# A down projection by seven half-sized products, its inputs combined while the up projection runs

## The chip, the cores and the metric

The kernel runs on one core of a Trainium2 chip. The metric is the device time of one execution in microseconds. The kernel before takes 2623.7 us, the median of 3 runs (2622.65 to 2625.96).

## What is computed

Two transformer blocks on 1024 tokens of 1024 features, float32. The first has a short-convolution layer and a stick-breaking attention layer, the second a sliding-window and a differential attention and then a feed-forward part. The change touches the end of the second block, D_FF = 2816:

```python
def _conv_ffn(h, w_up, conv_w, conv_b, w_down):
    u = h @ w_up
    a, g = jnp.split(u, 2, axis=-1)
    s = a.shape[1]
    ap = jnp.pad(a, ((0, 0), (CONV_WIDTH - 1, 0), (0, 0)))
    a = ap[:, 0:s] * conv_w[0] + ap[:, 1:s + 1] * conv_w[1] + ap[:, 2:s + 2] * conv_w[2] + conv_b
    return (jax.nn.gelu(a, approximate=False) * g) @ w_down
...
        h2 = _rmsnorm(x, norm2_g[l]) * (1.0 + scale2) + shift2
        x = x + gate2 * _conv_ffn(h2, w_up[l], conv_w[l], conv_b[l], w_down[l])
    return _rmsnorm(x, final_g)
```

## The kernel before

Activations lie feature-major: a tile is 128 features by 512 tokens, and there are two halves of tokens. Every operand of a projection is split into a high and a low part of type fp32r, so that one block product is three matrix products (high by high, high by low, low by high). Weights come in pieces of up to four 128 x 128 blocks: `Piece.load` fetches one on SP's queue (tile wr), `split_h` makes the high part on ACT (wh), `split_l` the low part on DVE (wl). All pieces stand in one list, `stream`, and `advance` (line 360) keeps loads, high and low parts a set number of pieces ahead of the piece in use: 5, 3 and 2, and 8, 5 and 4 in the down projection.

The order of all instructions is made beforehand by a planner written in the kernel, `Sched`: a main program on TensorE and side tasks (generators), each resumed when the planner's own clock says that what it waits for is there. Each engine and each DMA queue then works through its list in that order. `bank` hands out the eight PSUM banks, `big` and `sml` the tiles of two pools in SBUF (34 tiles of 4 KB and 32 of 2 KB a partition), and `room` (line 311) makes a task wait until a large tile is free by the planner's count.

The up projection is already made by seven products in place of eight (`up_first`, `up_rest`, line 1543). For it, `weight_sums` (line 1435) forms sums of quarters of the up weights in memory by accumulating DMAs on POOL's queue, one every 6 us of the planner's clock from 130 us on, with a pause from 600 to 880; each has a small copy ahead of it (tile paced) that reads the newest low part of a weight piece, and so keeps the DMA from running ahead of its place. `up_out` (line 1459) makes the convolution, the gelu (tile fa) and the product with the gate, and stores each result (22 feature blocks by 2 halves) to act_d by POOL's queue.

The down projection is eight half products in the plain way. `act_side` (line 1622) loads the inputs back (tile al, five ahead) and splits them into act; `res_jobs` (line 764) takes one output block of 128 features after the other, over 22 inner blocks: the first half of the tokens 512 wide, the second half in two passes of 256 tokens, so that the last output can start early. Each result is multiplied by the gate and added to the old x (tile xn). `final` (line 1640) transposes finished blocks (yt), sums squares (fj), and after the eighth block scales and writes the output rows (y).

## Time and profile before

| | |
|---|---|
| median of 3 runs | 2623.7 us |
| the profiled execution | 2622.0 us, of which the span of instructions is 2620.2 us |
| TensorE busy (products) | 2563.2 us, 98% |
| DVE busy | 1724.2 us, 66% |
| ACT busy | 1238.8 us, 47% |
| POOL busy | 333.0 us, 13% |
| mean granted TensorE clock | 0.996 of full speed |
| HBM read and written | 213 GB/s over the span |

The span is the time from the first to the last instruction of one profiled execution. Busy time is the time in which an engine had an instruction at work; products on TensorE overlap, so their durations add up to more than the time that they take together, and the spacing of their starts is what counts.

### The profile page before, as it was taken

To read this page: it belongs to the slowest core of one execution; us is meant where nothing else is said; L and a number is where in the kernel's file an instruction comes from. 1 tells how busy PE (TensorE), PEld (TensorE's weight loads), DVE (VectorE), ACT (ScalarE), POOL (GpSimd) and SP (SyncE) were. 2 spreads that over 40 slices of the span, in tenths; PEclk is the share of its full clock that TensorE was granted. 3 is DMA by queue.
4 is the path that set the end of the run, shared out by engine and by line. 5 is a ranking of instruction groups with operands and counts; after the bars stand their busy time and mean duration, and the time that the engine had idled before them with its cause. 6 is when DMAs were issued, how large, how long until landed. Compare 5 with 4: busy or idle time off the path is not lost.

```text
span 2620.2 us, 39902 instructions
## 1 busy us (share of the span) xinstructions
PE 2563.2 (98%) x14015; PEld 2118.3 (81%) x14015; DVE 1724.2 (66%) x3137; ACT 1238.8 (47%) x2498; POOL 333.0 (13%) x598
## 2 busy tenths in 40 slices
PE   7999999999999899999999999999999999999998
PEld 6888888889877677788778887888787788887898
DVE  7866666765466777977677456674657766763564
ACT  5311113542255667667675353565535444442443
POOL 0011112332100012322200110000001000000000
PEclk9999999999999999999999999999999999999999
DMA  8866878798776656875974758555454545545675
GB/s 278 263 190 208 213 218 286 210 285 263 240 200 191 212 173 143 241 241 147 245 200 126 231 152 226 164 157 168 154 162 154 169 145 178 163 126 168 191 230 156
DMA packets 536305, 515.19 MB, mean 197 GB/s; under 512 B 30110, under 2 KB 429736, under 8 KB 536104
## 3 DMA queue, kind: packets, MB, share of 16 engines
q1 hardware_dynamic: 497396, 377.27, 49.5%
q0 software_dynamic: 36352, 131.15, 16.7%
q10 hardware_dynamic: 2356, 4.21, 0.4%
q8 instruction: 111, 1.82, 0.3%
q14 instruction: 90, 0.74, 0.1%
HBM read 422.33 MB, written 136.31 MB: 213 GB/s over the span
## 4 chain that ended last, share of the span: by engine, by line
PE 87%; DVE 6%; issue 3%; DMA 2%; ACT 1%; SPq 0%; POOL 0%; DVEq 0%; ACTq 0%; POOLq 0%
PE pj L248 70%; PE z L248 4%; PE o L248 4%; PE pv L248 4%; PE tr L249 3%; DVE om L249 2%; DVE wl L249 1%; DVE be L249 1%; PE sm L249 1%; DVE act L249 1%; DMA wr<-in_b_w_qz_dram 1%; DVE t L249 0%; DMA wr<-in_b_w_out_dram 0%; DVE p L249 0%; SPq L249 0%
## 5 line engine op out<-in xcount | busy, mean ns | idle before, releaser
L248 PE MATMUL pj<-act,wh 128*128 128x512 f32 (+1 forms) x6064 | 1831.8, 386 | 6.7 <-DVE act L249 4.2
L248 PEld LDWEIGHTS pj<-act,wh 128*128 128x128 f32 x6064 | 1094.3, 189 | 221.5 <-DVE act L249 6.3
L248 PE MATMUL pj<-act,wl 128*128 128x512 f32 (+1 forms) x3032 | 1156.5, 381 | 1.4 <-DVE wl L249 1.4
L248 PEld LDWEIGHTS pj<-act,wl 128*128 128x128 f32 x3032 | 570.2, 188 | 122.5 <-DVE wl L249 2.7
L249 DVE TENSOR_TENSOR wl<-wr,wh 128x512 fp32r<-128x512 f32 (+1 forms) x752 | 494.5, 676 | 179.8 <-ACT wh L249 172.6
L249 ACT CAST wh<-wr 128x512 fp32r<-128x512 f32 (+1 forms) x752 | 445.4, 615 | 164.6 <-PE pj L248 83.5
L249 ACT COPY aT<-tr 128x512 f32<-128x512 f32 (+3 forms) x272 | 128.3, 501 | 163.7 <-PE tr L249 159.7
L248 PE MATMUL z<-kd,qs 128*128 128x256 f32 (+2 forms) x704 | 164.3, 351 | 0.1
L249 DVE SCALAR_TENSOR_TENSOR acc<-mw,silu_c,acc 128x512 f32<-128x512 f32 x196 | 146.6, 748 | 3.1 <-DMA mw<-in_a_mod_w_dram 0.3
L248 PE MATMUL pv<-wh,act 128*128 128x256 f32 x768 | 140.3, 282 | 0.0
L249 POOL COPY paced<-wl 128x1 f32<-128x1 f32 x128 | 67.2, 525 | 512.0 <-DVE wl L249 490.0
L248 PEld LDWEIGHTS z<-kd,qs 128*128 128x128 f32 x704 | 115.0, 192 | 17.1 <-issue 5.8
L249 DVE TENSOR_TENSOR_SCAN om<-om 128x640 f32<-128x640 f32 (+3 forms) x64 | 120.8, 1887 | 9.0 <-ACT om L249 9.0
L248 PEld LDWEIGHTS pv<-wh,act 128*128 128x128 f32 x768 | 119.1, 188 | 0.3
L249 DVE SCALAR_TENSOR_TENSOR xn<-pj,mod,xo 128x512 f32<-128x512 f32 (+1 forms) x40 | 25.7, 643 | 141.2 <-PE pj L248 141.2
L248 PEld LDWEIGHTS o<-aT,vp 128*64 128x64 f32 (+1 forms) x1440 | 97.5, 147 | 23.4 <-issue 12.6
L248 PE MATMUL o<-aT,vp 128*64 128x128 f32 (+1 forms) x1440 | 114.0, 278 | 1.7 <-ACT aT L249 1.7
L248 PE MATMUL pv<-wl,act 128*128 128x256 f32 x384 | 108.0, 281 | 0.3 <-DVE wl L249 0.3
L249 ACT ACTIVATE p<-p,t 128x256 f32<-128x256 f32 (+7 forms) x128 | 81.3, 636 | 22.5 <-DVE t L249 22.4
L249 ACT COPY u<-pj 128x512 f32<-128x512 f32 x38 | 22.3, 587 | 136.7 <-PE pj L248 69.9
L249 ACT ACTIVATE om<-z 128x384 f32<-128x384 f32 (+2 forms) x128 | 68.9, 539 | 22.3 <-PE z L248 22.0
L249 PE MATMUL tr<-ident,be 128*128 128x128 f32 x416 | 61.0, 281 | 18.2 <-DVE be L249 16.9
(226 smaller groups left out, 2408.6 us busy)
## 6 DMA issues: line engine op xcount, KB each, us to landing
wr<-in_w_in_dram SPq DMA_DIRECT2D x136, 256.0 KB
mw<-in_w_ada_dram SPq DMA_DIRECT2D x96, 256.0 KB
wr<-in_w_down_dram SPq DMA_DIRECT2D x96, 256.0 KB
wr<-in_a_w_in_dram SPq DMA_DIRECT2D x80, 256.0 KB
wr<-in_w_up_dram SPq DMA_DIRECT2D x66, 256.0 KB
wr<-in_b_w_qz_dram SPq DMA_DIRECT2D x64, 256.0 KB
qs<-q_d SPq DMA_DIRECT2D x64, 256.0 KB
mw<-in_a_mod_w_dram SPq DMA_DIRECT2D x48, 256.0 KB
```

The lines of the kernel that those rows point to most:

```text
L248: return f(out, *value, **kw)
L249: return f(out=out, **kw)
```

## The change

With the token halves 0 and 1, the inner halves 0 and 1 (11 feature blocks each) and the output halves 0 and 1 (4 blocks each), the down projection needs eight block products. The change forms seven (Strassen's scheme in Winograd's form). The seven inputs are stored in dn_d: kinds 0, 1 and 6 are results of `up_out` as they are; kinds 2 to 5 are sums and differences of four of them, made by the new side task `down_in` as soon as the three later ones of a block exist, by four DVE operations (the first input, long stored, is loaded back as dT). Four sums of weight quarters, sw_d, are made by `weight_sums` after those of the up weights, by 64 more DMAs of 176 x 512 numbers (352 KB, as before). `down` then runs the products in the order of `todo`: each over 4 output blocks and 11 inner blocks, the first six 512 tokens wide, the seventh in two passes of 256. Products 0 and 1, 2 to 4, and 5 and 6 share a PSUM bank for each output block, where they add up; partial results are taken out by DVE with the gate (or its negative) and the old x. The old `final` becomes three parts, called when four, seven and eight blocks of an output are there. Inputs are freed and split kind by kind (`act_side`; `N_DOWN` large tiles are kept for results that stay). Over the whole program there are 264 products of 256 columns where there were 1056, and 8304 of 512 columns in the projections where there were 8040.

```diff
-R_SUM = 64
 AHEAD_ACT = 5
+N_DOWN = 13
...
-    act_d = scratch("act_d", [NF, 128, S])
+    dn_d = [scratch(f"dn_d{i}", [NM, 128, HT]) for i in range(7)]
     s1_d = scratch("s1_d", [2, NM, 128, HT])
     sg_d = [[scratch(f"sg_d{i}{w}", [512, HF]) for w in "ag"] for i in range(4)]
+    sw_d = [scratch(f"sw_d{i}", [HF, 512]) for i in range(4)]
...
+    w_down = w_down_2[0]
+
     def weight_sums():
-        def W(k, f, n):
-            return w_up[512 * k:512 * k + 512, n * DFF + f * HF:n * DFF + (f + 1) * HF]
+        def up(n):
+            return lambda k, f: w_up[512 * k:512 * k + 512, n * DFF + f * HF:n * DFF + (f + 1) * HF]
+
+        def down(k, f):
+            return w_down[HF * k:HF * k + HF, 512 * f:512 * f + 512]
         paced = const.tile([128, 1], F32, name="paced")
         while sch.t < T_SUM:
             yield 2.0
-        for n in range(2):
-            g = [sg_d[i][n] for i in range(4)]
-            for to, of, op in ((0, W(0, 1, n), None), (2, W(0, 0, n), None), (0, W(1, 1, n), ALU.add),
-                               (2, W(0, 1, n), ALU.add), (1, W(0, 0, n), None), (3, W(1, 0, n), None),
+        for W, g in [(up(n), [sg_d[i][n] for i in range(4)]) for n in range(2)] + [(down, sw_d)]:
+            rows, width = g[0].shape
+            step = rows // 8
+            for to, of, op in ((0, W(0, 1), None), (2, W(0, 0), None), (0, W(1, 1), ALU.add),
+                               (2, W(0, 1), ALU.add), (1, W(0, 0), None), (3, W(1, 0), None),
                                (1, g[0], ALU.add), (3, g[1], ALU.add)):
-                for r in range(0, 512, R_SUM):
-                    kw = {"accum_op": op, "max_dma_last_dim": HF * 4} if op else {}
+                for r in range(0, rows, step):
+                    kw = {"accum_op": op, "max_dma_last_dim": width * 4} if op else {}
                     while BUSY_SUM[0] < sch.t < BUSY_SUM[1]:
                         yield 2.0
                     pol.tensor_copy(out=paced, in_=f32(stream[done_to["l"] - 1].l[:, 0, 0:1]))
-                    pol.dma_start(out=g[to][r:r + R_SUM], in_=of[r:r + R_SUM], **kw)
+                    pol.dma_start(out=g[to][r:r + step], in_=of[r:r + step], **kw)
                     yield E_SUM
     fhalo = const.tile([128, NF, 2], F32, name="fhalo")
     st_f = {}
+    st_d = {}
+
+    def down_in(i, h):
+
+        t1 = sml(name="dT1")
+        syn.dma_start(out=t1, in_=dn_d[0][i])
+        h01, h10, h11 = h[0, 1], h[1, 0], h[1, 1]
+        yield t1, h01, h10, h11
+        stt = vec.scalar_tensor_tensor
+        vec.tensor_tensor(out=t1, in0=t1, in1=h01, op=ALU.subtract)
+        vec.tensor_tensor(out=h01, in0=h11, in1=h01, op=ALU.subtract)
+        yield 0.5
+        t2 = sml(name="dT2")
+        stt(out=t2, in0=h11, scalar=-1.0, in1=t1, op0=ALU.mult, op1=ALU.subtract)
+        yield t2
+        t4 = sml(name="dT4")
+        stt(out=t4, in0=t2, scalar=-1.0, in1=h10, op0=ALU.mult, op1=ALU.subtract)
+        yield t4
+        for kind, t in ((2, t2), (3, h01), (4, t4), (5, t1)):
+            store(dn_d[kind][i], t)
+            flags.add(("dn", kind, i))
...
-            store(act_d[f, :, hs(half)], t)
-            flags.add(("act", f, half))
+            i = f % NM
+            if (f // NM, half) != (0, 1):
+                kind = {(0, 0): 0, (1, 0): 1, (1, 1): 6}[f // NM, half]
+                store(dn_d[kind][i], t)
+                flags.add(("dn", kind, i))
+            if (f // NM, half) != (0, 0):
+                got = st_d.setdefault(i, {})
+                got[f // NM, half] = t
+                if len(got) == 3:
+                    sch.spawn(down_in(i, st_d.pop(i)))
...
-    DOWN = [(0, 4), (NM, 4), (4, 4), (NM + 4, 4), (8, 3), (NM + 8, 3)]
-
-    def act_side(half):
-
-        fs = [f + i for f, n in DOWN for i in range(n)]
+
+
+    def act_side():
+
+        todo = [(kind, i) for kind in range(7) for i in range(NM)]
         got = {}
-        for k in range(NF + AHEAD_ACT):
-            if k < NF:
-                yield from wait(("act", fs[k], half))
-                got[k] = sml(name="al")
-                syn.dma_start(out=got[k], in_=act_d[fs[k], :, hs(half)])
-            if k >= AHEAD_ACT:
-                t = got.pop(k - AHEAD_ACT)
+        for n in range(len(todo) + AHEAD_ACT):
+            if n < len(todo):
+                yield from wait(("dn",) + todo[n])
+                got[n] = sml(name="al")
+                syn.dma_start(out=got[n], in_=dn_d[todo[n][0]][todo[n][1]])
+            if n >= AHEAD_ACT:
+                kind, i = todo[n - AHEAD_ACT]
+                t = got.pop(n - AHEAD_ACT)
                 yield t
+                if (kind, i) == (1, 0):
+                    yield from room(1, N_DOWN)
                 yield from room(1)
-                sch.spawn(split_to(("act", k - AHEAD_ACT, half), t))
+                sch.spawn(split_to(("dn", kind, i), t))
             yield 0.6
+    def down():
+        def of(s, j):
+            src, k0, c0 = [(w_down, 0, 0), (w_down, NM, 0), (sw_d[1], 0, 0), (sw_d[2], 0, 0), (w_down, NM, 512),
+                           (sw_d[0], 0, 0), (sw_d[3], 0, 0)][s]
+            return [Piece(src, k0 + k, n, c0 + j * 128, 128) for k, n in ((0, 4), (4, 4), (8, 3))]
+
+        todo = [(s, j, 0, HT, of(s, j)) for s in range(6) for j in range(4)]
+        todo += [(6, j, c0, 256, of(6, j)) for c0 in (0, 256) for j in range(4)]
+        for t in todo:
+            stream.extend(t[4])
+        stt = vec.scalar_tensor_tensor
+
+        def multiply(ps, pieces, kind, c, start, last):
+            k = 0
+            for pc in pieces:
+                use(pc)
+                for i in range(pc.nk):
+                    a = act_of(("dn", kind, k))
+                    sch.turn(sch.when((a, pc.h, pc.l)))
+                    first = start and k == 0
+                    for n, (w, x) in enumerate(((pc.h, 0), (pc.h, 1), (pc.l, 0))):
+                        mm(ps, lhsT=w[:, i, :], rhs=a[:, x, c], start=first and n == 0, stop=k == NM - 1 and n == 2,
+                           skip_group_check=not start)
+                    if last:
+                        del A["dn", kind, k]
+                        free()
+                    k += 1
+
+        two = {}
+
+        def old(f, half):
+            if (f // 2, half) not in two:
+                two[f // 2, half] = big([2, HT], name="xo", held=True)
+            t = two[f // 2, half][:, f % 2, :]
+            syn.dma_start(out=t, in_=x4_d[f, :, hs(half)])
+            return t
+
+        def scaled(out, ps, f, minus, plus):
+
+            g = V["gt2n" if minus else "gt2"][:, f:f + 1]
+            stt(out=out, in0=ps, scalar=g, in1=plus, op0=ALU.mult, op1=ALU.add)
+
+        def run():
+            V["gt2n"] = const.tile([128, 8], F32, name="gt2n")
+            vec.tensor_scalar(out=V["gt2n"], in0=V["gt2"], scalar1=-1.0, scalar2=None, op0=ALU.mult)
+            b, s1, zo, vo = {}, {}, {}, {}
+            xs = {0: [None] * 8, 1: [None] * 8}
+
+            def after(s, j, c0, xo):
+                ps = b[j]
+                if s == 0:
+                    s1[j] = copied(ps, "s1")
+                elif s == 2:
+                    vec.tensor_tensor(out=ps, in0=ps, in1=s1[j], op=ALU.add)
+                    yield xo
+                    scaled(xo, ps, j, False, xo)
+                    sch.keep(ps)
+                    zo[j] = xo
+                elif s == 3:
+                    yield xo
+                    scaled(xo, ps, 4 + j, True, xo)
+                    sch.keep(ps)
+                    vo[j] = xo
+                else:
+                    f, half, minus, plus = {1: (j, 0, False, xo), 4: (4 + j, 0, True, xo), 5: (4 + j, 1, True, vo.get(j)),
+                                            6: (j, 1, False, zo.get(j))}[s]
+                    if s == 6:
+                        x = sml(256, name="xn")
+                        scaled(x, ps[:, c0:c0 + 256], f, minus, plus[:, c0:c0 + 256])
+                        if c0 == 0:
+                            sch.keep(ps)
+                    else:
+                        x = plus
+                        scaled(x, ps, f, minus, plus)
+                        if s == 5:
+                            sch.keep(ps)
+                    xs[half][f] = x
+                    bs = range(4) if s != 6 else range(c0 // 128, c0 // 128 + 2)
+                    yield x
+                    if s in (1, 5) and j == 3:
+                        yield from final_a(half, xs[half], 4 * (s == 5))
+                    elif s in (4, 6) and j == 2:
+                        yield from final_b(half, xs[half], 4 * (s == 4), bs)
+                    elif s in (4, 6) and j == 3:
+                        yield from final_c(half, xs[half], 4 * (s == 4), bs)
+
+            for s, j, c0, w, pieces in todo:
+                old_of = {1: (j, 0), 2: (j, 1), 3: (4 + j, 1), 4: (4 + j, 0)}.get(s)
+                xo = old(*old_of) if old_of else None
+                start = s in (0, 2, 5)
+                if start:
+                    sch.turn(sch.bank_time())
+                    b[j] = bank("pj")
+                multiply(b[j][:, c0:c0 + w], pieces, s, slice(c0, c0 + w), start, j == 3 and c0 + w == HT)
+                then(after(s, j, c0, xo))
+        return run
+
...
+    def final_a(half, xs, f0):
+
+        f = final_state(half)
+        for b in range(4):
+            yield from sch.a_bank()
+            f["ps"][b] = bank("yt")
+            final_turn(f, xs, range(f0, f0 + 4), b, 0, 0)
+            f["y"][b] = big([D], name="y", held=True)
+            c = slice(f0 * 128, f0 * 128 + 512)
+            vec.tensor_tensor(out=f["y"][b][:, c], in0=f["ps"][b], in1=fin["g"][:, c], op=ALU.mult)
+
+    def final_b(half, xs, f0, bs):
+        f = final_state(half)
+        for b in bs:
+            yield from sch.a_bank()
+            f["ps"][b] = bank("yt")
+            final_turn(f, xs, range(f0, f0 + 3), b, bs[0] if len(bs) == 2 else 0, 1)
+
...
-    last = res_jobs(w_down_2[0], "act", "gt2", x4_d, None, final, ks=DOWN, squares=False)
-    run_last = [alone(last, 0)] + [alone(again(last), (1, c0, 256)) for c0 in (0, 256)]
+    run_last = down()
...
-        sch.spawn(act_side(0))
+        sch.spawn(act_side())
         run_up1()
-        sch.spawn(act_side(1), 60.0)
         ahead.update(load=AHEAD_LOAD + E_L, h=AHEAD_H + E_H, l=AHEAD_L + E_H)
-        for run in run_last:
-            run()
+        run_last()
```

What moves, first on SP's queue in one round of the up stage (wr are weight pieces, s1l a stored partial result, al an input of the down projection; dn_d_108 holds kind 1, dn_d_107 kind 0). Before:

```order
L249 DMA wr_21967<-sg_d3a 128x4x128
L249 DMA al_21983<-act_d 128x512
L249 DMA wr_21993<-sg_d2g 128x4x128
L249 DMA wr_22015<-sg_d0g 128x4x128
L249 DMA wr_22038<-sg_d1a 128x4x128
L249 DMA s1l_22059<-s_d 128x512
```

and now:

```order
L249 DMA wr_21918<-sg_d3a 128x4x128
L249 DMA al_21934<-dn_d_108 128x512
L249 DMA wr_21944<-sg_d2g 128x4x128
L249 DMA dT_4778_21964<-dn_d_107 128x512
L249 DMA wr_21967<-sg_d0g 128x4x128
L249 DMA wr_21990<-sg_d1a 128x4x128
L249 DMA s1l_22013<-s_d 128x512
```

The load of dT stands between the first weight pieces of the round, two places behind that of al.

On DVE in a round of the same stage (fa are results of the up projection, pj PSUM banks, u and v copies of them), before:

```order
L249 TENSOR_TENSOR pj_21645<-pj_21645,u_21567 128x512
L249 TENSOR_TENSOR fa_21617<-fa_21617,pj_21645 128x512
L249 TENSOR_TENSOR act_21740<-al_20790,act_21740 128x512
L249 TENSOR_TENSOR wl_21747<-wr_21669,wh_21714 128x512
L249 TENSOR_TENSOR act_21754<-al_21026,act_21754 128x512
L249 TENSOR_TENSOR act_21762<-al_21258,act_21762 128x512
L249 TENSOR_TENSOR act_21770<-al_21493,act_21770 128x512
L249 TENSOR_TENSOR wl_21784<-wr_21692,wh_21745 128x512
L249 TENSOR_TENSOR y_4767_21798<-pj_21779,v_21776 128x512
L249 TENSOR_TENSOR wl_21807<-wr_21712,wh_21782 128x512
L249 TENSOR_TENSOR pj_21802<-pj_21802,s1l_21569 128x512
```

and now:

```order
L249 TENSOR_TENSOR pj_21847<-pj_21847,u_21765 128x512
L249 TENSOR_TENSOR fa_21819<-fa_21819,pj_21847 128x512
L249 TENSOR_TENSOR wl_21948<-wr_21874,wh_21920 128x512
L249 TENSOR_TENSOR wl_21971<-wr_21898,wh_21946 128x512
L249 TENSOR_TENSOR y_4783_21985<-pj_21966,v_21962 128x512
L249 TENSOR_TENSOR wl_21994<-wr_21918,wh_21969 128x512
L249 TENSOR_TENSOR dT_4778_21964<-dT_4778_21964,fa_21819 128x512
L249 TENSOR_TENSOR fa_21819<-fa_21741,fa_21819 128x512
L249 TENSOR_TENSOR pj_21989<-pj_21989,s1l_21767 128x512
L249 TENSOR_TENSOR wl_22019<-wr_21944,wh_21992 128x512
```

The splits of act have gone from here, and the operations on dT (and fa from two fa) stand ahead of the addition of s1l, behind y.

On POOL's queue in mid-kernel, where the second block's first projections store keys and queries (ka_d, qa_d), before:

```order
L249 DMA g_d<-gt_15084 128x512
L249 DMA g_d<-gt_15125 128x512
L249 DMA ka_d<-ks_15165 128x512
L249 DMA ka_d<-ks_15166 128x512
L249 DMA qa_d<-qh_15255 128x512
L249 DMA qa_d<-ql_15256 128x512
L249 DMA qa_d<-qh_15298 128x512
```

and now:

```order
L249 DMA g_d<-gt_15175 128x512
L249 COPY paced<-wl_15226 128x1
L249 DMA sw_d_123<-in_w_down_dram 176x512
L249 DMA ka_d<-ks_15217 128x512
L249 DMA ka_d<-ks_15218 128x512
L249 COPY paced<-wl_15295 128x1
L249 DMA sw_d_123<-in_w_down_dram 176x512
L249 DMA qa_d<-qh_15311 128x512
L249 DMA qa_d<-ql_15312 128x512
L249 COPY paced<-wl_15340 128x1
L249 DMA sw_d_123<-in_w_down_dram 176x512
```

A paced copy and a DMA of the sums stand between the stores.

## Rows read from the trace of the kernel before

**Rows 1.** The page: busy times of the engines, and POOL's DMA queue.

```profile
PE 2563.2 (98%) x14015; PEld 2118.3 (81%) x14015; DVE 1724.2 (66%) x3137; ACT 1238.8 (47%) x2498; POOL 333.0 (13%) x598
...
q0 software_dynamic: 36352, 131.15, 16.7%
```

**Rows 2.** The chain of waits, 2040 to 2621 us: start, length, what.

```profile
2051.93 304.05 PE pj L248 x1308
...
2421.99 46.01 PE pj L248 x198
...
2484.79 31.19 PE pj L248 x264
```

**Rows 3.** Groups by shape, 2356 to 2611 us: busy us, mean ns, idle before.

```profile
L248 PE MATMUL pj<-act,wh 128*128 128x256 f32 x704 | 125.6, 281 | 0.0
L248 PE MATMUL pj<-act,wh 128*128 128x512 f32 x352 | 111.0, 395 | 0.4 <-DVE act L249 0.3
...
L248 PE MATMUL pj<-act,wl 128*128 128x256 f32 x352 | 98.8, 281 | 0.0
L248 PE MATMUL pj<-act,wl 128*128 128x512 f32 x176 | 69.4, 394 | 0.0
L249 DVE TENSOR_TENSOR wl<-wr,wh 128x512 fp32r<-128x512 f32 x94 | 59.8, 684 | 7.6 <-ACT wh L249 5.7 <-PE pj L248 1.9
...
L249 DVE SCALAR_TENSOR_TENSOR xn<-pj,mod,xo 128x256 f32<-128x256 f32 x15 | 7.2, 482 | 42.7 <-PE pj L248 42.7
```

**Rows 4.** Windows: length, busy us (instructions) by engine, clock, DMA share, GB/s.

```profile
300.00:600.00 300.00, 299.66 (x1391) 246.01 (x1390) 205.59 (x336) 102.81 (x178) 74.20 (x138) 1.00 0.86 250
900.00:1200.00 300.00, 284.36 (x2052) 232.35 (x2053) 242.19 (x285) 207.65 (x451) 70.84 (x108) 0.99 0.67 186
1260.00:1320.00 60.00, 60.00 (x372) 49.00 (x371) 37.09 (x120) 31.59 (x88) 17.58 (x34) 1.00 1.03 261
1320.00:1760.00 440.00, 434.70 (x2324) 359.92 (x2323) 292.08 (x737) 236.58 (x498) 35.98 (x65) 1.00 0.62 179
1440.00:1500.00 60.00, 60.00 (x300) 50.29 (x299) 29.81 (x46) 21.85 (x39) 10.95 (x20) 1.00 0.78 231
1560.00:1640.00 80.00, 79.12 (x396) 62.93 (x395) 53.88 (x130) 33.65 (x85) 3.79 (x7) 1.00 0.78 219
2200.00:2300.00 100.00, 100.00 (x433) 80.92 (x432) 68.02 (x118) 45.70 (x82) 5.40 (x10) 1.00 0.52 154
2356.00:2510.00 154.00, 153.60 (x791) 129.35 (x790) 75.53 (x134) 60.53 (x125) 4.87 (x9) 1.00 0.63 192
2510.00:2611.00 101.00, 101.00 (x858) 100.88 (x856) 49.54 (x96) 41.47 (x88) 2.14 (x4) 1.00 0.61 182
```

The engines in these rows are PE, PEld, DVE, ACT and POOL, in this order.

**Rows 5.** Groups by shape, 2000 to 2350 us: a sum of two tiles on DVE.

```profile
L249 DVE TENSOR_TENSOR T<-T,act 128x512 f32<-128x512 f32 x7 | 4.8, 693 | 0.2
```

**Rows 6.** Timeline of one up round, SP's queue, then DVE: start, length, what.

```profile
2154.10 0.36 SPq L249 DMA_DIRECT2D wr<-sg_d3a  x1
2164.35 0.81 SPq L249 DMA_DIRECT2D al<-act_d  x2
...
2169.41 0.69 DVE L249 TENSOR_TENSOR y<-pj,v 128x512 f32<-128x512 f32 x1 [0.60 <-PE pj L248]
```

**Rows 7.** Waits of SP's queue, 2000 to 2350 us: total, times, longest.

```profile
SPq L249 <- DMA act_d<-fa: 101.4, 14, 12.2
```

**Rows 8.** Instructions of act_d (stores) and of paced.

```profile
DMA to landing us min/median/max: 2.3/2.5/7.1
...
L249 POOL COPY paced<-wl x128: 183/426/2050, 143.0 to 1318.1; 128x1 f32<-128x1 f32 x128
```

**Rows 9.** DMA queues, 300 to 600 us, then 640 to 880: packets, MB, share.

```profile
q0 software_dynamic: 7457, 28.71, 36.5%
...
q0 software_dynamic: 3816, 12.63, 14.4%
```

**Rows 10.** Waits of TensorE, 900 to 1080 us: total, times, longest.

```profile
PE tr L249 <- DVE be L249: 13.0, 13, 2.6
```

More of the change, by code (lines that the diff above doesn't have):

```diff
@@ L782, in post @@
             s["x"].append(xn)
[L783 to L800 removed]
+            for a, g in enumerate([None, extra_g]):
+                if a and g is None:
+                    continue
+                yield xn
+                sq = sml(name="sq")
+                act(out=sq, in_=xn, func=ACTF.Square, scale=V[g][:, j:j + 1] if g else 1.0)
+                yield sq
+                if j == 0:
+                    s["acc"][a] = sq
+                else:
+                    vec.tensor_tensor(out=s["acc"][a], in0=s["acc"][a], in1=sq, op=ALU.add)
+            if j == 7:
+                yield s["acc"][0]
+                yield from done(half, st.pop(half))
         def job(j):
@@ L808, in fn @@
                 then(post(j, half, ps, xo))
[L809 removed]
+            return chunk(w, j * 128), fn
         return [job(j) for j in range(NJ)]
     RB = {}
[L813 removed]
     def norm_side(consume):
@@ new lines, in final_state, with final_turn @@
+        return fin.setdefault(half, {"ss": tiny(12), "y": [None] * 4, "ps": [None] * 4})
+    def final_turn(f, xs, fs, b, b0, part):
+        ps = f["ps"][b]
+        for k in fs:
+            ten.transpose(out=ps[:, k % 4 * 128:(k % 4 + 1) * 128], in_=xs[k][:, (b - b0) * 128:(b - b0 + 1) * 128],
+                          identity=ident)
+        c = slice(fs[0] % 4 * 128, (fs[-1] % 4 + 1) * 128)
+        sq = sml(name="fj")
+        i = 3 * b + part
+        act(out=sq[:, c], in_=ps[:, c], func=ACTF.Square, accum_out=f["ss"][:, i:i + 1])
+        sch.keep(ps)
@@ L1668, in final, with final_c @@
+    def final_c(half, xs, f0, bs):
+        f = final_state(half)
+        nb = len(bs)
+        for b in bs:
+            final_turn(f, xs, range(f0 + 3, f0 + 4), b, bs[0] if nb == 2 else 0, 2)
         v = tiny(nb)
-        vec.tensor_reduce(out=v, in_=f["ss"][:, 0:3 * nb].rearrange("p (b g) -> p b g", g=3), axis=AX.X, op=ALU.add)
+        vec.tensor_reduce(out=v, in_=f["ss"][:, 3 * bs[0]:3 * bs[0] + 3 * nb].rearrange("p (b g) -> p b g", g=3),
+                          axis=AX.X, op=ALU.add)
```

61 lines of the change are left out of this document (10 added, 51 removed).

## The prediction

> **What bounds the kernel now.** The page comes first [rows 1]: TensorE is busy 2563.2 of 2620.2 us, so nearly every microsecond is a number of matrix products times their spacing. The chain of waits says the same of the end [rows 2]: one piece of it is 1308 products of the up stage in a row. Next, the groups between 2356 and 2611 us, the down projection [rows 3]: 352 + 176 = 528 products of 512 columns for the first half of the tokens and 704 + 352 = 1056 of 256 columns for the second. This is what the change rewrites. The means in those rows (395 and 281 ns) overlap each other; the spacing is read from the chain [rows 2]: 198 wide products took 46.01 us, 0.2324 us each (in the up stage 304.05 / 1308 = 0.2325), and 264 narrow ones 31.19 us, 0.1181 us each. Check: 528 x 0.2324 + 1056 x 0.1181 = 122.7 + 124.7 = 247.4 us of the 255; the rest is 64 transposes and small gaps. The stage's windows show TensorE at 153.60 of 154 and 101.00 of 101 us and DVE at about half [rows 4]. So the down stage is bound by its products and by nothing else.
>
> **What goes.** Eight products of half size (halves of tokens, of inner blocks, of outputs) become seven. Each is 4 output blocks x 11 inner blocks x 3 matrix products = 132. Six run 512 wide, the seventh in two passes of 256: 792 wide and 264 narrow ones, so 264 wide more and 792 narrow fewer. 792 x 0.1181 - 264 x 0.2324 = 93.5 - 61.4 = **32.1 us** less on TensorE. The Trainium skill, in "TensorE: Matmul & The Clock Gate", section Back-to-back issue gap, gives about 131 ns for a product of 512 columns in a sustained stream; by that figure 132 products fewer would be worth an estimated 17 us. The rows disagree with it, and the rows decide. Weight pieces fall from 144 to 96 here, which takes some 33 us off DVE (684 ns each [rows 3]) that TensorE never waited for.
>
> **Added in the up stage.** In each of 11 rounds: a load on SP (the first product's input, back from memory), four DVE operations of 512 columns, three more stores on POOL. The nearest DVE row is 693 ns [rows 5]: 44 x 0.69 = 30 us, 2.8 a round. A round is 120 products, 27.9 us. DVE was busy 68.02 of 100 us between 2200 and 2300 with TensorE at 100.00 [rows 4], so its share rises to some 78% and there is cover; the question is the order. The new load (dT) stands on SP behind that of al, which already waits for a store: SP stood before it until 2164.35 us in the round shown [rows 6], and such waits were 101.4 us in 14 times, up to 12.2 [rows 7], without costing TensorE. dT is issued two places after al, at about 2165.7 on that clock. With 2.5 us to land, the median of these stores [rows 8] as the nearest row for a load, it is there at 2168.2. DVE comes to it after y, which waits for TensorE until 2169.41 [rows 6], and one wl: about 2170.7. So 2.5 us are to spare. Behind dT on DVE stands the addition of s1l; ACT copies its result, and TensorE needs that 24 other products (5.6 us) later. Bounds: not below nothing, since nothing is freed on the path here; above, if each load took 7.1 us, the longest landing [rows 8], DVE would stand 2.1 us a round, 23 us in 11 rounds if the 5.6 us hid none of it. I take 1.5 us, near the lower end, because SP's present waits in the same place are longer and cost nothing.
>
> **Added in mid-kernel.** The sums of the down weights: 64 more DMAs of 352 KB on POOL's queue, each behind a small copy (paced) that waits for a wl tile. The 128 for the up weights lie between 143.0 and 1318.1 us [rows 8]; less the 280 that the code's pause keeps free that is 7.0 us each, so the new ones fill about 1318 to 1760. TensorE is busy there 434.70 of 440 us, at a DMA share of 0.62 [rows 4]. Their price in DMA: POOL's queue takes 36.5% of the engines from 300 to 600, with 300 / 7.0 = 43 sums, and 14.4% from 640 to 880, in the pause [rows 9]. 22.1% of 300 us by 43 is 1.5 us of all engines a sum; 64 are 99 us, 0.22 over 440 us. The mean share goes to 0.84, in the two densest windows (0.78 each) to 1.00. From 300 to 600 the share was 0.86 with TensorE at 299.66 of 300; from 1260 to 1320 it was 1.03 with TensorE at 60.00 of 60, sums included [rows 4]. The loads' lead hides this much. But from here on the planner's order moves on every engine, and stores on POOL stand behind the paced copies. Below, at most the 5.3 us that TensorE lacks in those 440 could vanish; above, it could lose at the rate of 900 to 1200, where sums and attention ran together: 15.6 of 300 us [rows 4], which over 440 is 23, 18 more than now. I take 2 us: between 900 and 1080 the waits were for DVE's be inside attention (13.0 us [rows 10]), not for a DMA.
>
> **The down stage otherwise.** 33 more splits of inputs on DVE and ACT replace 48 splits of pieces. The first product's inputs are ready before the stage begins, and each later product has 30.7 us (132 x 0.2324) in which its eleven are made. Tight is the last narrow pass: in 132 x 0.1181 = 15.6 us DVE has 12 splits (8.2 at 0.684), 4 evictions (1.9 at 0.482 [rows 3]) and the output of the first two blocks, four operations of 512 columns and some small ones, at most 4 us by the same rows: 14.1 us. At worst those 4 us stand before a wl; at best they fill gaps. I take 1. The chain after the last product (transpose, square, root, scaling, output) has the same instructions as before.
>
> **Sum.** The profiled execution took 2622.0 us (span 2620.2): 2622.0 - 32.1 + 1.5 + 2 + 1 = 2594.4. The median of the runs stands 1.7 us above that execution, so **2596 us**.
>
> **Rivals.** (A) The up stage pays: store, al, dT, DVE, s1l come late in every round, 21 us more than I took: 2617 us. For it: SP does stand there in each round, and DVE gets its four operations at that very place. Against it: the 2.5 us to spare and the 5.6 us behind. (B) Mid-kernel loses at the rate of 900 to 1200, 16 us more: 2612. For it: new order, later stores. Against it: the waits named there. (C) Slower than before: the sums are dear. If all that POOL's queue takes (16.7% of the span [rows 1], 438 us) were the 128 sums, one would cost 3.4 us and 64 would add 0.50; the two windows at 0.78 (140 us) would want 1.28, and once the lead is used up weights would come 0.28 x 140 = 39 us late: 2596 + 39 = 2635. It decides where an added sum costs over about 3 us of all engines, for then the whole gain is given back. Against it: POOL's queue takes 14.4% without sums, which are plain stores. The Trainium skill, "DMA: Bandwidth & Descriptors", section Queues, rings and completion order, says that an engine takes turns between the queues with work, a packet at a time; by that rule a POOL queue that is never empty would leave weights half the engines. The row from 1260 to 1320 shows a full share and no loss. (D) The change does less than it says: the counts in the new order exclude that, 264 narrow products where 1056 stood.
>
> **Chances and range.** Forecast 0.78 (its own range 2588 to 2604: at one end no added cost and the 5.3 us gone, at the other the three costs nearly trebled), A 0.07, B 0.10, C 0.03, something else 0.02. The range reaches to B and leaves out A and C: 2587 to 2612. A measurement of this kernel can tell some 0.2%, 5 us, from no change. Forecast, A and B all lie under 2618, so faster 0.95; the same 0.02; slower 0.03.
>
> **What would show it.** Right: a down stage of about 223 us in place of 255, with spacings of 0.232 and 0.118 and TensorE over 99% busy; no loss of TensorE over 5 us in all between 2050 and 2350; the last sum near 1760 us; TensorE short of 1 to 10 us between 1320 and 1760. Wrong: TensorE waiting for wl behind a dT on DVE (A); idle inside attention after 1320 (B); waiting for wl or act behind a DMA in windows with a share over 1 (C).

## The result, and the profile after

The changed kernel takes **2590.1 us**, the median of 4 runs (2588.66 to 2590.88), against 2624.5 for the kernel before, the median of 4 runs: a ratio of 0.9869 with a 95% interval of 0.9852 to 0.9886, or 30 to 39 us less. The forecast was 2596 us with a range of 2587 to 2612; the time lies inside the range, 5.9 us below the forecast. The saving that it worked out came, and some 1.5 us more, and the 4.5 us that it set aside for added costs did not.

The profiled execution took 2590.8 us (span 2589.0, granted clock 0.996), 31.2 less than that of before. Its page, in the lines that answer to [rows 1]:

```profile
span 2589.0 us, 39065 instructions
...
PE 2533.8 (98%) x13487; PEld 2078.3 (80%) x13487; DVE 1752.3 (68%) x3175; ACT 1232.0 (48%) x2487; POOL 418.9 (16%) x759
...
q0 software_dynamic: 48720, 162.87, 21.9%
```

TensorE's busy time fell by 29.4 us; DVE's and POOL's rose by 28.1 and 85.9, POOL's queue moves more, and the span shrank. Then the chain of waits from 2040 us to the end (start, length, what), which answers to [rows 2]:

```profile
2053.32 0.71 DVE pj L249
...
2054.69 368.73 PE pj L248 x1587
2423.41 1.75 PE yt L249 x16
2425.16 82.85 PE pj L248 x357
...
2517.37 30.26 PE pj L248 x138
...
2549.38 11.62 PE pj L248 x99
...
2565.72 11.71 PE pj L248 x99
...
2580.25 0.49 DVE xn L249
```

The piece of products that ended with the up stage after 304.05 us [rows 2] now runs on into the down stage, 1587 products without a wait. The spacings are 368.73 / 1587 = 0.2323 us and, of the narrow ones, 11.62 / 99 = 0.1174 and 11.71 / 99 = 0.1183. The windows answer to [rows 4] (length, busy us and instructions of PE, PEld, DVE, ACT, POOL, then clock, DMA share, GB/s):

```profile
1320.00:1760.00 440.00, 434.73 (x2312) 360.21 (x2311) 291.27 (x736) 234.37 (x496) 104.19 (x195) 1.00 0.85 233
1440.00:1500.00 60.00, 60.00 (x287) 49.68 (x286) 32.72 (x51) 22.97 (x42) 22.76 (x39) 1.00 1.00 267
2060.00:2340.00 280.00, 280.00 (x1208) 226.56 (x1207) 204.00 (x351) 118.73 (x210) 30.07 (x56) 1.00 0.59 181
2480.00:2580.00 100.00, 100.00 (x587) 87.74 (x585) 57.14 (x110) 38.95 (x96) 6.91 (x12) 1.00 0.54 165
```

The added sums raise the DMA share of mid-kernel from 0.62 to 0.85, and TensorE is busy 434.73 us of it, where it was 434.70. In the up stage DVE went from 183.19 us of the same 280 before (65%) to 204.00 (73%), with TensorE busy throughout in both.

To place the difference, two events serve that both traces have: the last sum of up weights on POOL, up to which both programs have the same instructions in the same order, and the first and last addition of a stored partial result in the up stage. First the kernel before (name, count, duration in ns, first and last start), then after:

```profile
L249 POOL DMA_DIRECT2D sg_d3g<-sg_d1g x8: 781/808/1057, 1267.3 to 1318.5; - x8
...
L249 DVE TENSOR_TENSOR pj<-pj,s1l x22: 698/700/700, 2050.6 to 2339.3; 128x512 f32<-128x512 f32 x22
```

```profile
L249 POOL DMA_DIRECT2D sg_d3g<-sg_d1g x8: 781/807/1098, 1270.8 to 1321.1; - x8
...
L249 DVE TENSOR_TENSOR pj<-pj,s1l x22: 699/700/700, 2053.3 to 2341.9; 128x512 f32<-128x512 f32 x22
...
L249 POOL DMA_DIRECT2D sw_d<-in_w_down_dram x48: 545/565/1095, 1326.5 to 1641.8; - x48
L249 POOL DMA_DIRECT2D sw_d<-sw_d x16: 853/880/952, 1651.2 to 1753.2; - x16
```

| stretch, us | before | after | difference |
|---|---|---|---|
| start to the last sum of up weights | 1318.5 | 1321.1 | +2.6 |
| from there to the first addition of s1l | 732.1 | 732.2 | +0.1 |
| first to last addition of s1l (up stage, part of the next row) | 288.7 | 288.6 | -0.1 |
| first addition to the last product's end | 560.5 | 526.9 | -33.6 |
| last product's end to the end of the span | 9.15 | 8.8 | -0.35 |

The first row is no work of the change: nothing in it differs between the programs, and in the executions below the same event falls anywhere from 1317.4 to 1323.1 us. With these 2.6 us the 31.2 of the profiled pair become 33.8, close to the 34.4 of the medians. The gain lies wholly behind the up stage, and the two stretches in which work was added stayed as long as they were.

### The profile page after: what moved, and what is told of

Read it like the earlier page. It is cut to its first block, busy times and chain, and to the rows that moved or that the text cites. A ratio compares the mean times of both kernels' runs of the same rounds, so it can differ in the third digit from the quotient of the medians.

```text
span 2589.0 us, 39065 instructions
## 1 busy us (share of the span) xinstructions
PE 2533.8 (98%) x13487; PEld 2078.3 (80%) x13487; DVE 1752.3 (68%) x3175; ACT 1232.0 (48%) x2487; POOL 418.9 (16%) x759
## 3 DMA queue, kind: packets, MB, share of 16 engines
q10 hardware_dynamic: 2356, 4.21, 0.4%
## 4 chain that ended last, share of the span: by engine, by line
PE 54%; DVE 3%; ACT 1%; issue 0%; DMA 0%; DVEq 0%; ACTq 0%
PE pj L248 45%; PE o L248 3%; PE z L248 3%; PE tr L249 2%; PE pv L248 2%; DVE om L249 1%; DVE p L249 0%; DVE act L249 0%; DVE t L249 0%; DVE wl L249 0%; DVE be L249 0%; PE yt L249 0%; PE rb L249 0%; PE sm L249 0%; DVE fa L249 0%
## 5 line engine op out<-in xcount | busy, mean ns | idle before, releaser
L248 PE MATMUL pj<-act,wh 128*128 128x512 f32 (+1 forms) x5712 | 1794.4, 396 | 6.3 <-DVE act L249 2.9
L248 PEld LDWEIGHTS pj<-act,wh 128*128 128x128 f32 x5712 | 1047.7, 189 | 228.9 <-DVE act L249 4.4
L248 PE MATMUL pj<-act,wl 128*128 128x512 f32 (+1 forms) x2856 | 1117.8, 391 | 1.5 <-DVE wl L249 1.5
L248 PEld LDWEIGHTS pj<-act,wl 128*128 128x128 f32 x2856 | 537.7, 188 | 126.3 <-DVE wl L249 2.8
L249 DVE TENSOR_TENSOR wl<-wr,wh 128x512 fp32r<-128x512 f32 x704 | 468.8, 679 | 186.2 <-ACT wh L249 171.5
L249 ACT CAST wh<-wr 128x512 fp32r<-128x512 f32 x704 | 418.4, 617 | 132.6 <-PE pj L248 53.0
L249 POOL COPY paced<-wl 128x1 f32<-128x1 f32 x192 | 89.7, 467 | 694.4 <-DVE wl L249 646.9
L249 DVE TENSOR_REDUCE t<-sm 128x4 f32<-128x512 f32 x40 | 27.6, 691 | 80.2 <-PE sm L249 80.2
```

Source lines behind the costliest of these rows:

```text
L248: return f(out, *value, **kw)
L249: return f(out=out, **kw)
```

## The experiments

**Is it the eighth product?** Three runs change only the products of the down projection and, in e9 and e10, the size of the last outputs. In e4 the changed kernel does the first of its seven products twice over (132 wide products more), without a load, a split or an eviction more:

```diff
-                    for n, (w, x) in enumerate(((pc.h, 0), (pc.h, 1), (pc.l, 0))):
+                    for n, (w, x) in enumerate(((pc.h, 0), (pc.h, 1), (pc.l, 0)) * (2 if kind == 0 else 1)):
```

> The changed kernel with every matrix product of the first of the seven done twice, on the same weights and inputs: 132 products of 512 columns more, no load, split or store more; the output is not the reference's. Theory 'products': 132 x 0.2324 = 30.7 us more, 2621 us. Rival 'pieces' (the gain comes from 48 weight pieces fewer, with their loads and splits): far less than 30.7 us more, below 2605 us.

Measured: 2622.1 us, ratio to before 0.9988 (0.9979 to 0.9997); 32.0 us above the changed kernel. The piece of the chain in which they lie:

```profile
2052.27 399.33 PE pj L248 x1719
```

1719 - 1587 = 132 products more, and 399.33 - 368.73 = 30.6 us more. With all of the change's savings in pieces, loads and splits still in place, the gain is gone but for some 3 us (0.8 to 5.5 by the interval): it was TensorE's products, and no more than that is left for everything beside them.

In e10 the kernel before makes the second half of the tokens 512 wide, so that narrow and wide products can be told apart without the change:

```diff
-    run_last = [alone(last, 0)] + [alone(again(last), (1, c0, 256)) for c0 in (0, 256)]
+    run_last = [alone(last, 0), alone(again(last), 1)]
```

> The kernel before with the second half of the tokens of its down projection in one pass 512 wide for each output block in place of two passes of 256. 528 wide products take the place of 1056 narrow ones: 124.7 - 122.7 = 2.0 us less by the spacings. The tail after the last product is longer, by the 4 to 5 us that the changed kernel showed for its last product in one pass. Spacing theory: 2624.5 - 2.0 + 4.5 = 2627, so that narrow products are no loss worth the name and the gain is the eighth product. Rival: narrow passes cost more than their spacing (weight loads, DVE's evictions), and a part of the gain of the changed kernel is that it has fewer of them: under 2618.

Measured: 2627.9 us, ratio 1.001 (1.0001 to 1.0019), as the spacing theory has it: in the trace the stretch from the first addition of s1l to the last product's end is 557.8 us, 2.7 less than in the kernel before (2.0 were expected), and the tail behind it 14.3 in place of 9.15. So fewer narrow products are not where the gain is from; half a product in 512 columns costs within 3 us of what it costs in twice 256.

In e9 the seventh product of the changed kernel runs in one pass of 512:

```diff
-        todo += [(6, j, c0, 256, of(6, j)) for c0 in (0, 256) for j in range(4)]
+        todo += [(6, j, 0, HT, of(6, j)) for j in range(4)]
```

> The changed kernel with the seventh product in one pass of 512 columns in place of two of 256; the output stays the reference's. Products: 132 x 0.2324 = 30.7 us in place of 264 x 0.1181 = 31.2. Behind the last product stand four blocks of output in place of two: 2 x (0.49 + 0.74) on DVE, two more squares on ACT and two more transposes, 3.5 us. Expected 2593 us. If the two passes cost more than the spacing tells (the narrow price is wrong): 2588 us or less.

Measured: 2594.7 us, ratio 0.9887 (0.9873 to 0.9902), 4.6 above the changed kernel, where 3 were expected. The last result is taken out at 2576.44 and the span ends at 2590.0, 13.6 us later where two passes leave 8.8: the two passes are worth some 5 us, all in the tail.

**What do the additions cost by themselves?** In e3 the kernel before keeps its eight products and gets the sums of the down weights and `down_in` on top, its results stored and never used:

```diff
+    st_d = {}
+    def down_in(i, h):
...
+        syn.dma_start(out=t1, in_=act_d[i, :, hs(0)])
...
             store(act_d[f, :, hs(half)], t)
+            if (f // NM, half) != (0, 0):
...
+                    sch.spawn(down_in(i, st_d.pop(i)))
```

> The kernel before with both additions (sums of the down weights, combined inputs with their loads and stores) but with the old down projection of eight products, which uses neither. Theory 'hidden': the time of the kernel before, 2624.5 us within 3. Rival 'paid': 3.5 us more (2 in mid-kernel and 1.5 in the up stage), up to 2650 us by the upper bounds.

Measured: 2623.3 us, ratio 0.9996 (0.9987 to 1.0006). All the added work together costs nothing that can be measured (at most 1.6 us by the interval). e1 takes the sums of the down weights from the changed kernel, whose products then read quarters of the weights as they are:

```diff
-        for W, g in [(up(n), [sg_d[i][n] for i in range(4)]) for n in range(2)] + [(down, sw_d)]:
+        for W, g in [(up(n), [sg_d[i][n] for i in range(4)]) for n in range(2)]:
```

> The changed kernel without the 64 DMAs and copies that sum the down weights; products 2, 3, 5 and 6 use quarters of the down weights as they are in place of sums, so the output is not the reference's. Theory 'hidden': the sums cost nothing, the time is that of the changed kernel, 2590 us within 2, and TensorE is short of about 5 us between 1320 and 1760 as with them. Rival 'paid' (the 2 us of the prediction, or more): 2588 us or less, with TensorE's shortfall in 1320 to 1760 smaller by as much.

Measured: 2590.9 us, ratio 0.987 (0.9855 to 0.9885). Its window of mid-kernel:

```profile
1320.00:1760.00 440.00, 433.46 (x2320) 358.95 (x2319) 291.88 (x741) 236.99 (x503) 36.82 (x67) 1.00 0.61 180
```

The DMA share falls back to 0.61, and TensorE does not gain from it. e2 leaves out `down_in`, so that products 2 to 5 read other stored inputs:

```diff
-                if len(got) == 3:
-                    sch.spawn(down_in(i, st_d.pop(i)))
```

> The changed kernel without down_in: no dT load, no four DVE operations and no three more stores in each of 11 rounds of the up stage; products 2 to 5 read stored results as they are in place of sums and differences, so the output is not the reference's. Theory 'hidden': 2590 us within 2, the up stage from the first s1l addition to the end of its products as long as with them. Rival 'paid': 1.5 us less by the prediction, up to 23 us less by its upper bound.

Measured: 2589.7 us, ratio 0.9862 (0.9845 to 0.9878), the up stage 288.5 us from first to last s1l. e8 goes the other way and loads dT three times over, to push the very step that rival A rests on:

```diff
-        syn.dma_start(out=t1, in_=dn_d[0][i])
+        for _ in range(3):
+            syn.dma_start(out=t1, in_=dn_d[0][i])
```

> The changed kernel with the load of dT issued three times into the same tile, so that SP stands twice for a landing and dT comes some 5 us later in each of 11 rounds; the output stays the reference's. Theory 'cover': 2.5 us were to spare and 4 us of slack lie behind, so 2590 us within 3, DVE standing some 2 to 3 us a round at dT. Rival A: DVE's stand goes through to TensorE in each round, 11 x 2.5 = 27 us or more: 2617 us or more.

Measured: 2589.6 us, ratio 0.9872 (0.9855 to 0.9888). The waits of SP's queue and of DVE from 2060 to 2380 us and of TensorE from 2050 to 2420 (who, on what: total, times, longest):

```profile
SPq L249 <- DMA dT<-dn_d: 58.6, 22, 3.6
...
DVE dT L249 <- DMA dT<-dn_d: 1.7, 1, 1.7
...
PE pj L248 <- ACT u L249: 1.4, 1, 1.4
```

SP's queue stands 58.6 us for those loads, which it does not in the changed kernel. DVE waits for dT once, 1.7 us before 2094.05, less than this run was expected to show. TensorE's one wait ends at 2053.13, before any of these loads; it is the step through the first addition of s1l and u, which the kernels before and after take too. Rival A is out.

**How much more would DVE have hidden?** The same place, loaded with arithmetic. e7 forms two of the results of `down_in` seven times each (`n` = 6), e6 three times (`n` = 2):

```diff
+        for _ in range(n):
+            stt(out=t2, in0=h11, scalar=-1.0, in1=t1, op0=ALU.mult, op1=ALU.subtract)
         yield t2
...
+        for _ in range(n):
+            stt(out=t4, in0=t2, scalar=-1.0, in1=h10, op0=ALU.mult, op1=ALU.subtract)
         yield t4
```

> The changed kernel with twelve more DVE operations of 512 columns in each of the 11 rounds of the up stage (each of two of the four repeated six times with the same result, 0.69 us each, 8.2 us a round); the output stays the reference's. DVE was busy 204.00 of 280 us between 2060 and 2340, 20.3 us a round of 27.9. Theory 'cover' (DVE has room until its round is full): 28.5 us a round is 0.6 too much, 7 us in 11 rounds at the least, up to 30 with the bursts of 4 us standing before weight splits: 2597 to 2620 us. Rival A's sort of theory (each operation at that place is on the path): 11 x 8.2 = 90 us more, 2680 us.

> The first two of the four results that the combining task forms in a round of the up stage are each formed three times, four DVE operations more a round (2.75 us, 30 in 11 rounds). Cover theory, as corrected after the run with twelve more operations: what counts is how long the added burst is against the lead of the weight splits behind it; there, bursts of 5.04 us cost TensorE 4.7 us a round. A burst here is three operations, 2.1 us, under the two pieces of lead that the low parts have (a piece of four blocks is 12 products, 2.8 us). So TensorE loses nothing: 2588 to 2593 us. Rival, proportional: every us of added DVE time costs in the same ratio as there (51.5 us for 12 operations a round), a third of it for four: about 2607.

Measured: e7 2641.6 us, ratio 1.0069 (1.0054 to 1.0084), between what the two theories gave, so that neither had it; e6 2589.8, ratio 0.9869 (0.9852 to 0.9885), nothing lost, so that a price in proportion (2607) is out. The up stage's window, of e7 and then of e6:

```profile
2060.00:2340.00 280.00, 256.03 (x1032) 197.88 (x1030) 233.15 (x386) 103.45 (x183) 24.70 (x46) 0.96 0.50 154
```

```profile
2060.00:2340.00 280.00, 280.00 (x1209) 226.65 (x1209) 226.45 (x388) 118.96 (x210) 30.06 (x56) 1.00 0.58 181
```

DVE is busy 83% of the time in the one and 81% in the other, and TensorE stands 24 us in the one and not at all in the other. These shares do not tell the two apart, because e7's stage is itself longer: from the first to the last addition of s1l it takes 339.2 us, with 283.07 of them busy on DVE, and e6's takes 288.9 with 230.88. Against the 288.6 us of the changed kernel's stage, e7 asks DVE for 98% and e6 for 80%. Where in the round TensorE comes to stand is seen in DVE's list (e7, then e6: start, length, what):

```profile
2197.32 5.04 DVE L249 SCALAR_TENSOR_TENSOR dT<-fa,dT 128x512 f32<-128x512 f32 x7
```

```profile
2184.12 2.14 DVE L249 SCALAR_TENSOR_TENSOR dT<-dT,fa 128x512 f32<-128x512 f32 x3
2186.17 0.68 DVE L249 TENSOR_TENSOR wl<-wr,wh 128x512 fp32r<-128x512 f32 x1
```

Behind a burst of 2.14 us the next low part of a weight piece is made in time. Behind one of 5.04 us, longer than one piece of four blocks lasts on TensorE (12 x 0.2324 = 2.8 us), it is late, and TensorE waits for wl (until 2203.01 us) and, behind the next burst, for y (until 2213.34); in e7's waits from 2060 to 2420 us these are:

```profile
PE pj L248 <- DVE wl L249: 17.1, 21, 1.9
PE pj L248 <- DVE y L249: 12.8, 7, 2.4
```

So the waits stand right behind the bursts. But e7 has both the longer burst and nearly all of DVE's time, and no run spread the same work out in short pieces: which of the two costs the 51.5 us is not shown.

**Where do the sums begin to cost?** The sums of the down weights stood 6.8 us apart (the 64 of them from 1326.5 to 1753.2). e5 issues them every 1.5 us of the planner's clock, e11 every 3 (`E` = 1.5 and 3.0); on the chip that made one every 1.9 us (1327.0 to 1446.8) and one every 3.4 (1322.4 to 1538.1).

```diff
-                    yield E_SUM
+                    yield E_SUM if W is not down else E
```

> The changed kernel with the 64 sums of the down weights four times as close, one every 1.5 us of the planner's clock in place of 6, so that they crowd into about 100 us after 1320; the output stays the reference's. By the prediction's price (1.5 us of all DMA engines a sum) the share wanted there is the present 0.65 and 1.0 more. Theory 'excess', the mechanism of rival C: what is wanted over 1 makes weights late, 0.65 x 100 us less a lead of some 15 us, about 2640 us. Theory 'turns': weights want under half of the engines there and keep getting their turns beside a POOL queue that is never empty, so TensorE loses next to nothing, 2590 to 2594 us, and only the sums themselves land later.

> The changed kernel with the sums of the down weights issued every 3 us of the planner's clock in place of 6 (1.5 us cost 41 us). By the price of 1.5 us of all DMA engines a sum, one every 3.5 us adds 0.43: the mean share from 1320 to 1540 comes to about 1.05, in the two densest windows to 1.21. Excess theory (what the engines are asked for over a full share, and nothing else, comes late): 0.21 x 140 us of the dense windows is at most 29 us, of which the loads' lead takes some: 2592 to 2612. Rival, turns (a POOL queue that is never empty takes its share whatever the sum): as with the sums every 1.5 us, the loss sets in wherever the POOL queue is never empty: over 2615. Third: nothing shows until the queue's sums overlap three deep, 2588 to 2592.

Measured: e5 2631.4 us, ratio 1.0033 (1.0019 to 1.0046), the gain given back and 41 us lost against the changed kernel; e11 2608.8, ratio 0.9943 (0.9928 to 0.9959), 18.7 us lost. In e5 TensorE stands while the sums run, and ACT, which makes the high parts ahead of it, waits for weight loads (windows, then waits from 1320 to 1500 us):

```profile
1320.00:1380.00 60.00, 48.85 (x254) 39.88 (x253) 38.81 (x138) 37.45 (x93) 27.96 (x62) 0.89 1.01 292
1380.00:1440.00 60.00, 52.42 (x213) 40.44 (x214) 27.24 (x64) 22.72 (x46) 28.83 (x64) 0.85 1.06 263
```

```profile
ACT wh L249 <- DMA wr<-in_b_w_out_dram: 36.0, 7, 8.2
...
ACT wh L249 <- DMA wr<-in_w_in_dram: 19.5, 5, 7.4
...
PE pj L248 <- ACT wh L249: 8.2, 5, 2.6
PE pj L248 <- ACT act L249: 5.8, 2, 5.4
PE pj L248 <- DVE wl L249: 5.6, 3, 2.1
```

That is the mechanism of rival C, with its place: weights that land late once their lead is used up. But e11 does not look like that at all. Its windows where the sums run and, over 300 us after the last of them, at the end of attention:

```profile
1320.00:1560.00 240.00, 234.28 (x1233) 195.71 (x1232) 143.44 (x352) 127.43 (x263) 89.23 (x173) 0.99 0.98 268
1840.00:1900.00 60.00, 43.84 (x236) 37.25 (x235) 39.25 (x105) 34.76 (x59) 1.08 (x2) 0.86 0.16 53
```

and the same two of the changed kernel:

```profile
1320.00:1560.00 240.00, 234.80 (x1259) 195.26 (x1258) 151.30 (x392) 131.66 (x285) 61.23 (x116) 1.00 0.81 223
1840.00:1900.00 60.00, 56.03 (x280) 46.83 (x279) 36.60 (x77) 33.15 (x55) 3.76 (x7) 0.97 0.46 146
```

While the sums ran, TensorE lost half a microsecond at a DMA share of 0.98. It stands 16.2 us in a stretch with a share of 0.16, where the changed kernel stands 4.0. So the last run, e12, keeps the order of every instruction of e11 and takes the traffic away: each sum's DMA moves 8 rows in place of 176, and the planner is told the old size.

```diff
+                    n = 8 if W is down else step
+                    sch.times = step // n
-                    pol.dma_start(out=g[to][r:r + step], in_=of[r:r + step], **kw)
+                    pol.dma_start(out=g[to][r:r + n], in_=of[r:r + n], **kw)
+                    sch.times = 1
```

> The kernel with the sums of the down weights every 3 us lost 18.7 us against the changed one in the medians, yet its trace has TensorE at 234.28 of 240 us while the sums run (234.80 in the changed kernel), and lacks 16.2 us between 1840 and 1900, over 300 us after the last sum, where the changed kernel lacks 4.0. This kernel keeps every instruction of every engine in that very order, with each of the 64 sum DMAs cut from 176 rows to 8 (the sums are not formed; the products concerned read quarters of the down weights as they are). Order theory: the loss is the planner's other order, in which attention's last pieces have no products left beside them: still 2605 to 2612 us, TensorE lacking some 16 us between 1840 and 1900. Rival, DMA: the loss is the load on the DMA engines: 2588 to 2594 us. In between, each has a part.

Measured: 2610.6 us, ratio 0.9951 (0.9934 to 0.9968). The loss stays without the traffic. Its windows:

```profile
1320.00:1560.00 240.00, 234.77 (x1221) 196.57 (x1220) 145.90 (x364) 126.68 (x266) 85.80 (x175) 0.99 0.62 179
1840.00:1900.00 60.00, 43.83 (x249) 37.78 (x248) 37.35 (x102) 35.50 (x61) 2.16 (x4) 0.87 0.20 66
```

The stretch from the last sum of up weights to the first addition of s1l sets the kernels side by side:

| kernel | sums of down weights | stretch, us |
|---|---|---|
| before; e1 | none | 732.1; 732.6 |
| after; e3 | one per 6.8 us | 732.2; 731.6 |
| e11 | one per 3.4 us | 751.7 |
| e12 | in e11's order, 8 rows of 176 | 751.7 |
| e5 | one per 1.9 us | 773.7 |

e11 and e12 agree to 0.1 us, and in their traces TensorE, DVE and POOL go through the same instructions in the same order: at one sum in 3.4 us the traffic costs nothing and the order 19.5 us. What the order does can be read from TensorE's groups by shape between 1840 and 1900 us, in the changed kernel and then in e11:

```profile
L248 PE MATMUL pj<-act,wh 128*128 128x512 f32 x122 | 39.7, 407 | 0.0
```

```profile
L248 PE MATMUL pj<-act,wh 128*128 128x512 f32 x34 | 11.7, 427 | 0.0
...
L249 PE MATMUL tr<-ident,p 128*128 128x128 f32 x41 | 8.4, 373 | 6.9 <-DVE p L249 6.7 <-DVE t L249 0.2
```

The projections' products that stand between the pieces of attention in the one had been used up earlier in the other, so the last pieces have nothing beside them and TensorE waits on DVE's p and t (tiles of attention). The idle time of these 60 us is 12.2 more than in the changed kernel. Over the whole stretch of the table TensorE stands 24.2 us in e11 and 10.7 in the changed kernel, 13.4 more, and is busy 727.5 us in place of 721.5 with the same products, 6.1 more. The granted clock agrees with the latter: an estimated 0.14 x 43.84 - 0.03 x 56.03 = 4.5 us between 1840 and 1900 (0.86 against 0.97) and 0.03 x 54.30 = 1.6 between 1320 and 1380 (0.97 against 1.00).

For e5 order and traffic were not separated in this way. At the end of attention (1900 to 1960 us in this run) TensorE lacks 4.0 us, as in the changed kernel, so its 41.5 us lie elsewhere. They are 23.8 us more of standing and 17.7 more of busy time; an estimated 18.8 us of the kind come from the granted clock of 0.89, 0.85 and 0.89 in the three windows from 1320 to 1500. The waits of ACT name DMAs; how much of them a new order adds is open. No run was faster than the changed kernel beyond the measurement, so there is no better version to show.

## Why the prediction was right, step by step

**What goes.** Right: 32.1 us from the spacings of the chain, against 33.6 in that stretch of the trace, and 30.6 for 132 products put back (e4). Of the 1.5 us beyond the 32.1, some 0.9 stand in the trace of before at the start of its down stage, where TensorE comes twice upon an input (act) that is just being made (start, length, what):

```profile
2367.68 0.40 PE L248 MATMUL pj<-act,wh 128*128 128x512 f32 x1
2368.41 0.50 PE L248 MATMUL pj<-act,wh 128*128 128x512 f32 x1 [0.34 <-DVE act L249]
...
2370.37 0.95 PE L248 MATMUL pj<-act,wh 128*128 128x512 f32 x2
```

The first two start 0.73 us apart in place of 0.23, the one after them 0.34 behind, and the pair at 2370.37 takes 0.95 where others take 0.63. The piece of 1587 products goes through that point without a break; no run tested this by itself, and the other 0.6 us are not placed. On the spacing, the Trainium skill, "TensorE: Matmul & The Clock Gate", section Back-to-back issue gap, gives some 131 ns for a product of 512 columns in a sustained stream; the runs do not agree: they show 0.2323 us each over 1587 products in a row and 30.6 us for 132 of them.

**Up stage, 1.5 us.** It was 0: 288.7 and 288.6 us. The argument that SP's longer waits in the same place were harmless held, and e8 shows how far. What the prediction priced as the danger, the arrival of dT, was none, though a load takes longer than the 2.5 us that it took from the stores: 2.3 to 5.8 us, 3.9 in the median. DVE comes to dT 4.2 to 9.0 us after its issue and never waits for it. DVE's share between 2200 and 2300 us went from 68.02% to 73.93%, not to 78, for six splits of act (4.0 us) left this window as 16 new operations (10.9 us) came in. Three times the loads (e8) and twice the added operations (e6) cost nothing; twelve more operations a round do (e7).

**Mid-kernel, 2 us.** It was 0.1. The term was mis-sized: it stood for waits behind crowded queues, and the runs showed none. The price of a sum itself held. It was 1.5 us of all engines by rows of before. e11 and e12 differ in 37.4% of the engines on POOL's queue from 1320 to 1560 us (55.1% against 17.7%), and 0.374 x 240 / 64 = 1.4 us, an estimate. The last sum was issued at 1753.2 us, as forecast near 1760, and TensorE was short of 5.3 us in mid-kernel, inside the 1 to 10 given, but short of the same 5.3 before.

**Down stage otherwise, 1 us.** It was 0: TensorE is busy 100.00 of the last 100 us, so the last narrow pass, in which DVE was thought to be tight, was hidden. The stage begins at 2356.0 us before, 305.4 behind the first addition of s1l; from the same place after, 2358.7, to the end of the last product it took 221.5 us, where 223 was forecast.

**Rivals.** A is excluded by e2, e3 and e8. B was given 0.10, for idle time inside attention by the new order. It did not happen, yet e11 and e12 show that it is real, and at 19.5 us near the 18 that the prediction priced it at (2 us and 16 more). That it did not happen is in part luck: the order that the planner made for one sum every 6 us happened to leave the end of attention as it was, and the order for one every 3 us did not. The waits that the prediction named against it (DVE's be) said nothing of that; only a run did. C was put at 0.03 by the price of a sum; e5 shows its mechanism at work with cheap sums, when they come thick, though how much of e5's loss it makes is open: the chance stood for the rate that the change has. The Trainium skill's rule of turns ("DMA: Bandwidth & Descriptors", section Queues, rings and completion order), that an engine serves the queues with work a packet at a time, bears on this. From 1320 to 1560 us POOL's queue took 55.1% of the engines in e11 and SP's 42.4%, close to the 43.5% that SP's took in e12 beside 17.7% of POOL's, and the traffic cost nothing; from 1320 to 1500 us in e5 it was 60.7% against 34.9%, with weights late. No run shows the turns themselves.

## What to carry to other kernels

Where TensorE runs without a gap, an edit is worth the products that it removes times the spacing that the chain shows; check it by putting the products back and nothing else. Whether added work on another engine is hidden is not read from the engine's mean share alone: set its work against the length that the stage has without it, and look at the longest burst that stands ahead of the next operand. And where a planner makes the order, a change of rate is two changes: repeat the order with the work taken out of it before blaming the work.

## What was not expected

In e11 a DMA share of 0.98 over 240 us, and of 1.08 in one window of 60 us with TensorE at 60.00, cost nothing: e12, with a share of 0.62 in the same 240 us, loses as much. The window:

```profile
1500.00:1560.00 60.00, 60.00 (x357) 51.44 (x357) 25.25 (x63) 25.30 (x58) 22.24 (x39) 1.00 1.08 262
```

And the stretch without work cost more than its idle time. In e11 TensorE was busy 11.04 and then 14.11 of 20 us:

```profile
1860.00:1880.00 20.00, 11.04 (x60) 9.11 (x58) 14.63 (x45) 13.05 (x24) 0.00 (x0) 0.83 0.07 24
1880.00:1900.00 20.00, 14.11 (x70) 12.44 (x71) 8.76 (x22) 8.82 (x15) 0.00 (x0) 0.74 0.06 15
```

The granted clock of these two was 0.83 and 0.74, so a part of them ran at the lower of the two levels, 1.2 in place of 2.4 GHz; in the 20 us behind, with products again, it was 1.00.
